# Attention logits in alternating row groups, with pairs of PSUM banks that also take the transposed probabilities

## Chip, cores, metric

One core of a Trainium2 chip. The metric is the device time of one execution in microseconds (us), and the number compared is the median over runs.

## What is computed

Two stacks of two layers each, on 256 tokens of 1024 channels in float32. The first stack mixes by three attentions (A: top-k by index scores, B: sliding window with sinks, C: stick-breaking), each with its own projections; the second works on two streams, x and a context c, with four mixers (A: a gated linear scan in both directions, B: dense GQA, C: differential attention, D: windowed GQA with sinks). The second layer of the second stack gives out only x. Cut to the parts that the change touches:

```python
def diff_attention(q, k, v, lam, lam_init, subln_g):       # mixer C: q, k [.., heads, 2, 32]
    scale = q.shape[-1] ** -0.5
    def block(qb):
        logits = jnp.einsum('bqhmd,bthmd->bhmqt', qb, k) * scale
        p = jax.nn.softmax(logits, axis=-1)
        w = p[:, :, 0] - lam * p[:, :, 1]
        return jnp.einsum('bhqt,bthd->bqhd', w, v)
...
def global_gqa(q, k, v, sink=None):                        # mixers B, D: heads of 64 channels
        logits = jnp.einsum('bqkgd,btkd->bkgqt', qb, k) * scale
        p = jax.nn.softmax(logits, axis=-1)                # with a sink: one more column
        return jnp.einsum('bkgqt,btkd->bqkgd', p, v)
...
def step(s, xs):                                           # mixer A: the scan
        att = jnp.einsum('bthk,bshk,btshk->bhts', qf, kf, decay)
        o = jnp.einsum('bthk,bkhv->bthv', qf * jnp.exp(bcum), s) + jnp.einsum('bhts,bshv->bthv', att, vf)
```

## The kernel before

Everything is in one class, `Net`. The residual streams lie channel-major. The large projections split their operands into a high and a low part (`split`, L111 on ScalarE and L112 on VectorE; tiles `wh`, `wl` of the weights, names such as `uh`/`ul`, `hxh`/`hxl`, `hch`/`hcl` of the activations) and take three products; `proj_tok` and `proj_ch` send 48 matmuls of 256 columns into one PSUM tile. These matmuls use the whole 128x128 array in one pass each. All other products are float32 and take two passes, which the trace shows as two records for each matmul.

PSUM has eight banks, in four pools: `pj` (3, projections), `lg` (2, logits and other short products), `tr` (2, transposes), `py` (1, the attention outputs). `mm` (L104) issues a matmul, `T` (L108) a transpose on TensorE.

A head has 64 channels, so its operands lie on partitions 0 to 63 or 64 to 127: the upper or the lower half of TensorE's rows, here called row group 0 and row group 1. An attention does, for one head or a few: the logits into an `lg` bank, for A, B and D with a mask added by one more matmul; `probs` (L397 the row maximum on VectorE, L402 exp with its sum on ScalarE); `weights_t` (L608 reciprocal, L610 scaling, transposes into a `tr` bank, L617 the copy `pt` to SBUF); then the products with the values into the `py` bank. It finishes one head (or the heads of one row group) before it begins the next. Mixer C has heads of two maps with 32 channels each: `diff` multiplies the queries by a mask (`qz`, L921) so that a product over all 128 rows gives one map's logits, combines both maps (L931 to L933), and transposes in `p_times_v` (copy `pt` at L412).

The scan (`gla`, L753 on) goes over levels b = 1, 2, 4 .. 128. A level copies the keys (`kc`, L794), does its products (`small` for b up to 16 in blocks of 32 columns, 128 columns above), picks values out of PSUM (L779, L811), and multiplies `QT`, `KT` and `FT` for the next level (L827, L829, L832).

A scheduler in the framework orders the instructions of every engine from its own estimates, so an edit at one place may move the rest. It runs waiting projections between the steps of attention and scan, as far as PSUM tiles are free.

Of the kernel before, what the change touches and what calls it, by code (L numbers as in the profile page):

```python
# [8 lines left out]
F32 = mybir.dt.float32  # L9
# [3 lines left out]
AF = mybir.ActivationFunctionType  # L13
# [14 lines left out]
def _ap(t, base, dims):  # L28
# [5 lines left out]
       ("cs32", (2, 2, 32)), ("dmask", (4,)))  # L34
# [24 lines left out]
class Net:  # L59
    """Residual streams are kept channel-major, [128 channels, 8, 256 tokens].  Operands of the large products are  # L60
    float32 values split exactly into two float32r parts (high, low); a product takes high*high + high*low + low*high."""
# [3 lines left out]
    def __init__(self, ctx, tc, I):  # L65
# [12 lines left out]
        self.tr = pool("tr", 2, space=ps)  # L78
# [6 lines left out]
    # ---------------------------------------------------------------- tiles  # L85
# [9 lines left out]

    def halves(self, name, tags):
        """a [128, 8, 256] tile in two pieces"""
        return Halves([self.K(name, [128, 4, 256], tag=t) for t in tags])
# [15 lines left out]
    # ------------------------------------------------------------ constants  # L114
    def load_consts(self):
# [9 lines left out]
        # 2 * silu of the conditioning vectors (ada halves its sums)  # L125
# [17 lines left out]
    def more_consts(self):  # L143
# [34 lines left out]
        # -lambda of the differential attention, per layer  # L178
# [13 lines left out]
        # forget gate lower bounds -> f = A + B * tanh(z / 2)  # L192
# [30 lines left out]
    def wtile(self, ap, c0, n=256, kt=8, pre=None):  # L223
        """columns c0..c0+n of ap [kt*128, N], split: w[part](k) -> [128, n]"""
# [16 lines left out]
    def fill(self, n, tags):  # L241
        """waiting jobs for a stretch in which the streams' chain leaves TensorE idle; their weights go to idle tags"""
# [5 lines left out]
    def proj_tok(self, w, n, u):  # L248
        """u (split, [128, 8, 256]) times w -> [128 tok, 2, n]"""
# [9 lines left out]
    def proj_ch(self, w, u, kt=8):  # L259
        """w (256 columns) times u -> [128 ch, 2, 256 tok]"""  # L260
# [9 lines left out]
    # --------------------------------------------------------------- pieces  # L270
    def ada(self, l, blk):
        """the modulation vectors, channel-major [128, 24, nv], and the jobs that fill them"""
# [9 lines left out]
        def job(n, ws=None):  # L282
# [8 lines left out]
            pc = self.P(self.tr, [128, 2, 4, 32])  # L291
# [9 lines left out]
    def chan_sum(self, x, square=False):  # L301
        """sums over channels of x [128, 8, 256] (or of its square), in four parts: rows 32 * g"""
        p = self.P(self.lg, [128, 512])
# [10 lines left out]
    def mean_row(self, x):  # L314
        """channel sums on every partition"""
        sb = self.chan_sum(x)
        p = self.P(self.lg, [128, 512])
# [3 lines left out]
    def rstd_row(self, x, eps):  # L321
        """(mean of x ** 2 over channels + eps) ** -0.5 on every partition"""
        V = self.nc.vector
        sb = self.chan_sum(x, True)
        p = self.P(self.lg, [128, 512])
# [13 lines left out]
    def log_exp(self, ins):  # L339
        """behind ins, ScalarE's tables hold both functions"""  # L340
# [4 lines left out]
    def rstd_small(self, r, ss):  # L345
        """(ss / 64 + eps) ** -0.5 of a few columns"""
# [3 lines left out]
    def rope(self, dst, src, H, cs, D=64, axial=False, dup=False):  # L350
        """src [128, 2, >=H*D] (PSUM or SBUF), dst [128, 2, H(, 2), D]; cs [128, 2 tok tiles, (cos, sin), D]"""
# [37 lines left out]
    def probs(self, hs, L, logits, nm, ss, nsink=None):  # L389
# [3 lines left out]
        p = self.P(self.lg, [128, nh, L])  # L393
        logits(p)
# [10 lines left out]
    def p_times_v(self, e, L, y, v):  # L405
# [25 lines left out]
    def affine_split(self, h, l, x, scale, bias, r=None):  # L431
        """split of x * scale (* r) + bias; scale and bias per channel, r per token"""
# [10 lines left out]
    def block1(self, l, xT, mod, pre):  # L443
# [18 lines left out]
        # ---- index scores, mixer A  # L462
# [24 lines left out]
        for t in range(2):  # L487
            L = 128 * (t + 1)
            S = self.W("score", [128, 256])[:, :L]
            rl = self.K("relu", [128, 4, 256], tag="at")  # L490
            for a in range(2):
                p = self.P(self.lg, [128, 2, 256])
                b = 64 * a
                for j in range(2):
                    self.mm(p[:, j, :L], iqT[b:b + 64, j, t * 128:t * 128 + 128], iqT[b:b + 64, 2, :L])
                A.activation(rl[:, a::2, :L], p[:, :, :L], AF.Relu)
# [32 lines left out]
        # ---- mixer C  # L529
# [10 lines left out]
        # ---- mixer B  # L540
# [49 lines left out]
    def finish1(self, ys, gT, Y):  # L590
        """gated and split"""
# [6 lines left out]
    def weights_t(self, e, hs, L, nm, ss, sink=None):  # L598
        """probabilities of heads hs from e [128 t, nh, L], transposed: [128 s, nh * L / 128, 128 t]"""
# [11 lines left out]
        p = self.P(self.tr, [128, 4, 128])  # L611
# [8 lines left out]
    def causal_softmax(self, H, tags, qT, kT, v, mask, sink=None, nsink=None):  # L620
        """causal tiles of 128 queries; mask(t) [128, L] additive bf16; -> [128 (head, channel), 4, 128 tok] each"""
        ys = []
        for t in range(2):
# [5 lines left out]
            for g in range(0, H // nh, 2):  # L629
                pts = []  # L630
                for a in range(2):
                    h0 = a + nh * g
                    hs = list(range(h0, h0 + 2 * nh, 2))

                    def logits(p):
                        for j, h in enumerate(hs):
                            b = 64 * (h % 2)
                            self.mm(p[:, j, :], qT[b:b + 64, h // 2, t * 128:t * 128 + 128], kT(h)[:, :L],
                                    start=j == 0, stop=False)
                        self.mm(p, self.identb, m[:, None, :L].to_broadcast([128, nh, L]), start=False, stop=True)  # L640
                    e = self.probs(hs, L, logits, nm, ss, nsink)
                    pts.append(self.weights_t(e, hs, L, nm, ss, sink))
# [10 lines left out]
    def stick(self, qT, kT, v, g, Y):  # L653
        """stick-breaking attention in [s, t] layout"""
        nc, V, A = self.nc, self.nc.vector, self.nc.scalar
        sl = [(slice(None), slice(None), slice(128 * s, 256)) for s in range(2)]
        for q in range(2):
            es = self.K("ste", [128, 4, 2, 256], tag="at")
            for a in range(2):
                b = 64 * a  # L660
                ps = []
                x = self.K("stx", [128, 768], tag=("s3", "n2")[a])
                xs = [x[:, :512].rearrange("p (j t) -> p j t", j=2), x[:, 512:].rearrange("p (j t) -> p j t", j=2)]
                for s in range(2):
                    p = self.P(self.lg, [128, 2, 256])
# [6 lines left out]
                    ps.append(p)  # L672
# [39 lines left out]
    def residual(self, n, r, g, b, name):  # L712
        """ALPHA * (n * r * g + b), put aside in DRAM until the layer's end"""
# [19 lines left out]
    def norm_layer(self, x):  # L733
        """x -> x - mean over channels; returns the rstd row"""
# [7 lines left out]
    def forget(self, l, d, p, FT, KT):  # L742
        """d: 0 forward, 1 backward; p [128, 2, 256] pre-activations"""
# [638 lines left out]
```

## Time and profile before

| | |
|---|---|
| runs (us) | 1384.69, 1383.55, 1381.17; median 1383.55 |
| profiled execution, span | 1377.40 us, one core, mean granted clock 0.986 |
| TensorE busy | 1330.4 us (97%) |
| VectorE / ScalarE / GpSimd busy | 844.3 (61%) / 655.1 (48%) / 25.4 us (2%) |
| DMA | 205.07 MB, 149 GB/s mean |

The span runs from the first to the last instruction of the profiled execution; the median of the runs is 6.15 us above it, and no device time beside the span was recorded for that execution. A busy time counts an engine as busy from an instruction's recorded start to its recorded end; on TensorE these overlap, and the recorded start of a matmul that follows another shape of tile lies ahead of the work. The distance between two starts therefore says more than a duration there.

### The profile page before, as it was taken

The numbers are of one execution on the slowest core, as the hardware profiler recorded it, in microseconds if no ns is written. First come the engines' busy times: TensorE is split into PE (matmuls) and PEld (weight loads), VectorE is DVE, ScalarE is ACT, GpSimd is POOL, SyncE is SP. The second block draws the span as 40 slices with busy tenths as digits, with TensorE's granted clock in tenths as the row PEclk, the third lists the DMA queues.
The fourth block names the chain that finished last, engine by engine and source line by source line (L and its number), as shares of the span: only waits on it lengthen the run. The fifth ranks groups of instructions, "written<-read, shape, count | busy, mean of one in ns | idle before, by whom it ended". The sixth has DMA issues, their size and how long they took to land.

```text
span 1377.4 us, 27990 instructions
## 1 busy us (share of the span) xinstructions
PE 1330.4 (97%) x11682; PEld 1164.2 (85%) x11682; DVE 844.3 (61%) x1744; ACT 655.1 (48%) x1178; POOL 25.4 (2%) x23
## 2 busy tenths in 40 slices
PE   5999999999999999999998999999999998999996
PEld 2998987899889898789998989977877788997774
DVE  3795454655559544565576366756577777775764
ACT  3455555544444545654443233346455546534652
POOL 0000000000000000000000000000000000000000
PEclk9899999999999999999999999999999999999998
DMA  9754746568746474547764442322143355522111
GB/s 330 216 151 131 232 142 190 158 204 266 227 124 184 123 212 141 153 138 220 211 214 153 135 142 63 109 93 77 52 139 118 107 154 159 175 81 62 62 62 46
DMA packets 199214, 205.07 MB, mean 149 GB/s; under 512 B 8368, under 2 KB 197424, under 8 KB 198448
## 3 DMA queue, kind: packets, MB, share of 16 engines
q1 hardware_dynamic: 199088, 203.28, 48.3%
q8 instruction: 92, 1.51, 0.4%
q14 instruction: 34, 0.28, 0.1%
HBM read 199.06 MB, written 4.19 MB: 148 GB/s over the span
## 4 chain that ended last, share of the span: by engine, by line
PE 82%; DMA 6%; DVE 4%; issue 4%; ACT 2%; SPq 1%; POOL 0%; POOLq 0%; ACTq 0%; DVEq 0%
PE ps L104 77%; PE ps L108 5%; DMA wr<-w_in 4%; DMA wsp<-w_ada 2%; DVE wl L112 2%; ACT wh L111 1%; SPq L219 1%; DMA wr<-w_out 0%; DMA cT<-ctx 0%; DVE KTc L829 0%; DVE af L439 0%; ACT Xx L1305 0%; ACT pe L402 0%; ACT L566 0%; DVE QTc L827 0%
## 5 line engine op out<-in xcount | busy, mean ns | idle before, releaser
L112 DVE TENSOR_TENSOR wl<-wr,wh 128x1024 fp32r<-128x1024 f32 (+1 forms) x270 | 328.4, 1217 | 258.3 <-ACT wh L111 255.8
L111 ACT ACTIVATE wh<-wr 128x1024 fp32r<-128x1024 f32 (+1 forms) x270 | 284.6, 1055 | 378.2 <-PE ps L104 255.2
L104 PE MATMUL ps<-uh,wh 128*128 128x256 f32 x704 | 202.2, 287 | 2.4 <-ACT thm L566 2.4
L104 PE MATMUL ps<-ul,wh 128*128 128x256 f32 x704 | 200.9, 285 | 0.0
L104 PE MATMUL ps<-uh,wl 128*128 128x256 f32 x704 | 200.8, 285 | 0.0
L104 PEld LDWEIGHTS ps<-uh,wh 128*128 128x128 f32 x704 | 132.7, 188 | 8.2 <-issue 4.4
L104 PEld LDWEIGHTS ps<-ul,wh 128*128 128x128 f32 x704 | 132.8, 189 | 1.9 <-issue 1.7
L104 PEld LDWEIGHTS ps<-uh,wl 128*128 128x128 f32 x704 | 132.7, 188 | 1.9 <-issue 1.6
L104 PE MATMUL ps<-wh,uh 128*128 128x256 f32 (+1 forms) x416 | 120.2, 291 | 2.0 <-ACT uh L440 1.2
L104 PE MATMUL ps<-wl,uh 128*128 128x256 f32 (+1 forms) x416 | 119.9, 289 | 1.0 <-DVE wl L112 1.0
L104 PE MATMUL ps<-wh,ul 128*128 128x256 f32 (+1 forms) x416 | 120.0, 289 | 0.1
L402 ACT ACTIVATE pe<-ps,nm 128x512 f32<-128x512 f32 (+2 forms) x160 | 84.9, 539 | 54.4 <-DVE nm L397 41.1
L397 DVE TENSOR_REDUCE nm<-ps 128x1 f32<-128x512 f32 (+2 forms) x104 | 71.1, 687 | 42.2 <-PE ps L104 42.0
L104 PEld LDWEIGHTS ps<-wh,uh 128*128 128x128 f32 x416 | 81.2, 196 | 4.1 <-ACT uh L440 1.4
L104 PEld LDWEIGHTS ps<-wl,uh 128*128 128x128 f32 x416 | 81.3, 196 | 1.8 <-DVE wl L112 1.3
L104 PEld LDWEIGHTS ps<-wh,ul 128*128 128x128 f32 x416 | 81.5, 196 | 1.2 <-DVE ul L441 0.9
L104 PE MATMUL ps<-wh,hxh 128*128 128x256 f32 x256 | 72.4, 283 | 0.0
L104 PE MATMUL ps<-wh,hxl 128*128 128x256 f32 x256 | 72.1, 281 | 0.0
L104 PE MATMUL ps<-wl,hxh 128*128 128x256 f32 x256 | 72.0, 281 | 0.0
L104 PE MATMUL ps<-hxh,wh 128*128 128x256 f32 x224 | 64.9, 294 | 4.2 <-ACT hxh L440 4.2
L104 PE MATMUL ps<-hxl,wh 128*128 128x256 f32 x224 | 64.6, 290 | 2.7 <-DVE hxl L441 2.7
L104 PE MATMUL ps<-hxh,wl 128*128 128x256 f32 x224 | 64.6, 290 | 0.6 <-DVE wl L112 0.6
(351 smaller groups left out, 3150.7 us busy)
## 6 DMA issues: line engine op xcount, KB each, us to landing
wr<-w_in SPq DMA_DIRECT2D x204, 512.0 KB, 4.0
wsp<-w_ada SPq DMA_DIRECT2D x68, 512.0 KB, 5.7
wr<-w_out SPq DMA_DIRECT2D x40, 512.0 KB, 3.7
wr<-w_ada SPq DMA_DIRECT2D x28, 512.0 KB, 3.9
wr<-w_br_a SPq DMA_DIRECT2D x8, 512.0 KB, 3.9
wr<-w_br_c SPq DMA_DIRECT2D x8, 512.0 KB, 4.6
wr<-w_br_b SPq DMA_DIRECT2D x8, 512.0 KB, 4.6
Xx<-resx SPq DMA_DIRECT2D x2, 1024.0 KB, 4.7
```

The source lines that it names most:

```text
L104: self.nc.tensor.matmul(o, l, r, start=start, stop=stop, skip_group_check=True)
L108: self.nc.tensor.transpose(o, i, self.ident[:n, :n])
L111: self.nc.scalar.activation(h, x, AF.Copy)
L112: self.nc.vector.tensor_tensor(l, x, h, op=OP.subtract)
L219: self.nc.sync.dma_start(out=w[:, :, :n], in_=ap[k0 * 128:k0 * 128 + 512, c0:c0 + n].rearrange("(k p) n -> p k n", p=128))
L397: nc.vector.tensor_reduce(nmx, p, axis=AX.X, op=OP.max, negate=True)
L402: nc.scalar.activation(e[:, j, :], p[:, j, :], AF.Exp, bias=nm[:, h:h + 1], accum_out=ss[:, h:h + 1])
```

## The change

The pool `tr` is gone, and `lg` has two tiles of two banks each (`P2`). `banks` issues the logits of the row groups alternately, each group into its own bank, and the masks behind them. The probabilities are transposed into the bank that held their own logits (`blocks`). The other users of `tr` (`tok_to_ch`, `finish2`, the modulation vectors in `ada`, the scan's state tiles) take tiles of `pj`. `chan_sum`, `mean_row` and `rstd_row` take a pair and use one half. Mixer C's queries are no longer masked: each map's logits use 32 rows, and the scale 32 ** -0.5 goes into the copy of the queries in `tok_to_ch`. Maps of 256 keys, which shared a bank, now have one each. In the scan, the loop over row groups becomes the inner one.

```diff
+    def P2(self, *shape):
+        t = self.lg.tile([128, 2, 512], F32, name="pp")
...
-        self.tr = pool("tr", 2, space=ps)
...
     def tok_to_ch(self, dst, src, scale=1.0, n=2):
-        p = self.P(self.tr, [128, 2, 2, 128])
+        p = self.P(self.pj, [128, 2, 2, 128])
...
+    def banks(self, nh, L, q, k, mask=None):
+        ps = self.P2(nh, L)
+        for j in range(nh):
+            for a, p in enumerate(ps):
+                self.mm(p[:, j, :], q(a, j), k(a, j), start=j == 0, stop=mask is None)
+        if mask is not None:
+            for p in ps:
+                o, m = mask(p)
+                self.mm(o, self.identb, m, start=False, stop=True)
+        return ps
...
-    def weights_t(self, e, hs, L, nm, ss, sink=None):
+    def weights_t(self, e, hs, L, nm, ss, p, sink=None):
...
-        p = self.P(self.tr, [128, 4, 128])
+        p = self.blocks(p)
...
     def small(lhs, rh, first, mask):
-            for a in range(2):
-                p = self.P(self.lg, [128, 2, 2, 32])
-                for ct in range(2):
-                    for t in range(2):
+            ps = self.P2(2, 2, 32)
+            for ct in range(2):
+                for t in range(2):
+                    for a in range(2):
...
             for h in range(4):
-                qz = self.W("qz", [128, 2, 128])
...
-                V.tensor_tensor(qz, qT[:, ct:ct + 1, t * 128:t * 128 + 128].to_broadcast([128, 2, 128]),
-                                self.dmask[:, mo:mo + 2, None].to_broadcast([128, 2, 128]), op=OP.mult)
...
+                rows = [slice(64 * (h % 2) + 32 * m, 64 * (h % 2) + 32 * m + 32) for m in range(2)]
+                ps = self.banks(1, L, lambda m, j: qT[rows[m], ct, t * 128:t * 128 + 128],
+                                lambda m, j: kT[rows[m], ct, k0:k0 + L])
+                es = [self.probs([2 * h + m], L, ps[m], nm, ss)[:, 0] for m in range(2)]
```

On TensorE, at the end of mixer C of the last layer (`pe` are probabilities, `pt` the SBUF copy of their transpose, `vC` values, `kC` keys, `qz` the masked and `qC` the plain queries). Before:

```order
L104 MATMUL ps_14629<-vC_14147,pt_14735 128x64 x4
L104 MATMUL ps_14800<-kC_13165,qz_14798 128x512
L108 MATMUL ps_14760<-ident_111,pe_14749 128x128 x4
L104 MATMUL ps_14805<-kC_13165,qz_14798 128x512
L104 MATMUL ps_14629<-vC_14147,pt_14765 128x64 x4
L104 MATMUL ps_14827<-kC_13165,qz_14825 128x512
L108 MATMUL ps_14787<-ident_111,pe_14776 128x128 x4
```

The change, in the same place:

```order
L117 MATMUL pp_14585<-kC_13020,qC_13846 128x512 x2
L121 MATMUL pp_14562<-ident_108,pe_14566 128x128 x4
L117 MATMUL ps_14463<-vC_13993,pt_14579 128x64 x4
L117 MATMUL pp_14608<-kC_13020,qC_13846 128x512 x2
L121 MATMUL pp_14585<-ident_108,pe_14589 128x128 x4
L117 MATMUL ps_14463<-vC_13993,pt_14602 128x64 x4
```

The two maps' logits stand together now, and the product with the values (`vC,pt_14579`) stands right behind the transposes of the same probabilities (`pp_14562`, which `pt_14579` is copied from), where a logits product stood between.

On TensorE, the scan of x in the last layer (`QTx`, `kc`: queries and copied keys; `wh`, `hch`, `hxh` and the like: projections). Before, a level:

```order
L104 MATMUL ps<-wh,hch 128x256
L104 MATMUL ps<-wh,hcl 128x256
L104 MATMUL ps<-wl,hch 128x256
L104 MATMUL ps<-QTx,kc 32x32 x32
L104 MATMUL ps<-wh,hch 128x256
L104 MATMUL ps<-wh,hcl 128x256
```

The change:

```order
L117 MATMUL ps<-wh,hxh 128x256
L117 MATMUL ps<-wh,hxl 128x256
L117 MATMUL ps<-wl,hxh 128x256
L117 MATMUL pp<-QTx,kc 32x32 x119
L121 MATMUL ps<-ident,ro 128x128 x4
L117 MATMUL ps<-wh,hxh 128x256
```

A level has 32 such products. Before, projections stand between any two levels; now three levels and most of a fourth stand in a row, and the rest of that fourth with two more behind the projections that follow (a row of 73).

## Rows read from the trace of the kernel before

**Rows 1.** The page: busy time, share of the span and instructions of each engine.
```profile
PE 1330.4 (97%) x11682; PEld 1164.2 (85%) x11682; DVE 844.3 (61%) x1744; ACT 655.1 (48%) x1178; POOL 25.4 (2%) x23
```

**Rows 2.** Stretches: length, busy PE, PEld, DVE, ACT, POOL (instructions), granted clock, DMA share, GB/s.
```profile
0.00:40.00 40.00, 24.69 (x186) 11.60 (x187) 18.32 (x71) 15.00 (x28) 0.91 (x5) 0.89 1.01 327
...
600.00:640.00 40.00, 40.00 (x350) 38.00 (x349) 20.96 (x31) 17.76 (x24) 0.00 (x0) 1.00 0.60 180
...
1200.00:1240.00 40.00, 40.00 (x557) 37.15 (x555) 29.80 (x60) 14.15 (x22) 0.00 (x0) 1.00 0.29 83
...
1280.00:1320.00 40.00, 39.71 (x237) 28.37 (x236) 31.23 (x83) 24.00 (x59) 1.81 (x1) 1.00 0.17 54
```

**Rows 3.** Timeline of PE around logits of 512 keys, 64 rows: start, us, what.
```profile
916.42 0.28 PE L104 MATMUL ps<-hcl,wh 128*128 128x256 f32 x1
916.63 1.12 PE L104 MATMUL ps<-kB,qB 64*128 64x512 f32 x2
917.68 0.39 PE L104 MATMUL ps<-hch,wl 128*128 128x256 f32 x1
917.91 0.28 PE L104 MATMUL ps<-hch,wh 128*128 128x256 f32 x1
```

**Rows 4.** Timeline of PE: logits of 256 keys (three, then two), projections between.
```profile
904.84 1.13 PE L104 MATMUL ps<-kB,qB 64*128 64x256 f32 x6
905.91 1.05 PE L104 MATMUL ps<-wr,cs 128*32 128x256 f32 x10
...
907.23 0.28 PE L104 MATMUL ps<-hch,wl 128*128 128x256 f32 x1
...
909.47 0.28 PE L104 MATMUL ps<-hch,wh 128*128 128x256 f32 x1
909.68 1.13 PE L104 MATMUL ps<-kB,qB 64*128 64x256 f32 x4
910.74 0.39 PE L104 MATMUL ps<-hcl,wh 128*128 128x256 f32 x1
```

**Rows 5.** Timeline of PE at mixer C, last layer, masked queries, and the transposes.
```profile
1288.04 1.02 PE L104 MATMUL ps<-kC,qz 128*128 128x512 f32 x2
1288.89 1.00 PE L104 MATMUL ps<-vC,pt 128*128 128x64 f32 x8
1289.73 0.61 PE L108 MATMUL ps<-ident,pe 128*128 128x128 f32 x4
```

**Rows 6.** Timeline of PE, one level of the scan.
```profile
1206.90 0.28 PE L104 MATMUL ps<-wl,hch 128*128 128x256 f32 x1
1207.11 0.76 PE L104 MATMUL ps<-QTx,kc 64*32 64x32 f32 x64
1207.80 0.38 PE L104 MATMUL ps<-wh,hch 128*128 128x256 f32 x1
1208.02 0.28 PE L104 MATMUL ps<-wh,hcl 128*128 128x256 f32 x1
```

**Rows 7.** Timeline of DVE behind a level of the scan (its products start at 1212.76).
```profile
1213.29 0.60 DVE L779 COPY_PREDICATED gc<-c_gmask,ps 128x128 f32<-128x128 uint8 x2 [2.31 <-PE ps L104]
1213.79 0.68 DVE L827 TENSOR_TENSOR QTx<-QTx,FTx 128x512 f32<-128x512 f32 x1
1214.51 0.28 DVE L832 TENSOR_TENSOR FTx<-FTx 128x64 f32<-128x64 f32 x1
1214.89 0.69 DVE L829 TENSOR_TENSOR KTx<-KTx,FTx 128x512 f32<-128x512 f32 x1
```

**Rows 8.** Timeline of DVE and ACT (two answers) between logits and products, mixer C, last layer.
```profile
1289.09 0.69 DVE L397 TENSOR_REDUCE nm<-ps 128x1 f32<-128x512 f32 x1 [1.07 <-PE ps L104]
...
1291.08 0.75 DVE L933 SCALAR_TENSOR_TENSOR pe<-pe,dc 128x512 f32<-128x512 f32 x1
...
1289.82 0.69 ACT L402 ACTIVATE pe<-ps,nm 128x512 f32<-128x512 f32 x1 [2.01 <-DVE nm L397]
...
1290.50 0.59 ACT L412 ACTIVATE pt<-ps 128x512 f32<-128x512 f32 x1
```

More of the change, by code (lines that the diff above doesn't have):

```diff
@@ L94, in P @@
         return pool.tile(shape, dt, name="ps")
+    def P2(self, *shape):
+        t = self.lg.tile([128, 2, 512], F32, name="pp")
+        n = math.prod(shape)
+        out = []
+        for a in range(2):
+            v = t[:, a, :n]
+            if len(shape) == 2:
+                v = v.rearrange("p (a b) -> p a b", a=shape[0])
+            elif len(shape) == 3:
+                v = v.rearrange("p (a b c) -> p a b c", a=shape[0], b=shape[1])
+            out.append(v)
+        return out
     def halves(self, name, tags):
@@ L403, in probs, with blocks, p_times_v @@
         return e
-    def p_times_v(self, e, L, y, v):
+    @staticmethod
+    def blocks(p):
+        return _ap(p, p, [[128, 4], [1, 128]])
+    def p_times_v(self, e, L, y, v, p):
         nst = L // 128
-        p = self.P(self.tr, [128, 4, 128])
+        p = self.blocks(p)
         for s in range(nst):
@@ L490, in block1 @@
             rl = self.K("relu", [128, 4, 256], tag="at")
-            for a in range(2):
[L492 to L496, printed above, removed]
+            ps = self.P2(2, 256)
+            for j in range(2):
+                for a in range(2):
+                    b = 64 * a
+                    self.mm(ps[a][:, j, :L], iqT[b:b + 64, j, t * 128:t * 128 + 128], iqT[b:b + 64, 2, :L])
+            for a in range(2):
+                A.activation(rl[:, a::2, :L], ps[a][:, :, :L], AF.Relu)
             V.tensor_scalar(S, rl[:, 0, :L], iws[:, t, 0:1], None, op0=OP.mult)
@@ L633, in causal_softmax @@
                     hs = list(range(h0, h0 + 2 * nh, 2))
[L635 to L642, printed above, removed]
+                    e = self.probs(hs, L, ps[a], nm, ss, nsink)
+                    pts.append(self.weights_t(e, hs, L, nm, ss, ps[a], sink))
                 for j in range(nh):
@@ L798, in gla @@
             elif out:
-                for a in range(2):
-                    p = self.P(self.lg, [128, 2, 2, 128])
-                    for ct in range(2):
-                        for t in range(2):
+                ps = self.P2(2, 2, 128)
+                for ct in range(2):
+                    for t in range(2):
+                        for a, p in enumerate(ps):
                             h = 2 * ct + a
@@ L809, in gla @@
                                         QT[64 * a:64 * a + 64, 1 - t, ct, 128 * (1 - t):128 * (1 - t) + 128])
+                for a, p in enumerate(ps):
                     if b < 128:
@@ L889, in gqa @@
             pts = {}
-            for hs in ([[0, 2], [1, 3]] if nh == 2 else [[h] for h in range(4)]):
-                def logits(p):
-                    for j, h in enumerate(hs):
-                        b = 64 * (h % 2)
-                        self.mm(p[:, j, :], qT[b:b + 64, h // 2, t * 128:t * 128 + 128],
-                                kT[b:b + 64, h // 2, k0:k0 + L], start=j == 0, stop=masks is None)
-                    if masks is not None:
-                        m, st = masks[t]
-                        self.mm(p[:, :, 128 * st:128 * st + 128], self.identb, m, start=False, stop=True)
-                e = self.probs(hs, L, logits, nm, ss, nsink)
-                pt = self.weights_t(e, hs, L, nm, ss, sink)
-                for j, h in enumerate(hs):
-                    pts[h] = pt[:, j * nst:j * nst + nst]
-                if h % 2:
-                    for c in range(h // 2 if nh == 1 else 0, h // 2 + 1):
-                        for s in range(nst):
-                            for a in range(2):
-                                self.mm(y[64 * a:64 * a + 64, c, 128 * t:128 * t + 128], v(c, s),
-                                        pts[2 * c + a][:, s], start=s == 0, stop=s == nst - 1)
+            mask = None
+            if masks is not None:
+                m, st = masks[t]
+                mask = lambda p: (p[:, :, 128 * st:128 * st + 128], m)
+            for cs in ([[0, 1]] if nh == 2 else [[0], [1]]):
+                ps = self.banks(nh, L, lambda a, j: qT[64 * a:64 * a + 64, cs[j], t * 128:t * 128 + 128],
+                                lambda a, j: kT[64 * a:64 * a + 64, cs[j], k0:k0 + L], mask)
+                for a in range(2):
+                    hs = [2 * c + a for c in cs]
+                    e = self.probs(hs, L, ps[a], nm, ss, nsink)
+                    pt = self.weights_t(e, hs, L, nm, ss, ps[a], sink)
+                    for j, h in enumerate(hs):
+                        pts[h] = pt[:, j * nst:j * nst + nst]
+                for c in cs:
+                    for s in range(nst):
+                        for a in range(2):
+                            self.mm(y[64 * a:64 * a + 64, c, 128 * t:128 * t + 128], v(c, s),
+                                    pts[2 * c + a][:, s], start=s == 0, stop=s == nst - 1)
         self.nc.scalar.activation(ys().rearrange("p (c n) -> p c n", c=2), y, AF.Copy)
@@ L1079, in qk_c @@
                 A.activation(f2(ro), p, AF.Copy)
-            self.tok_to_ch(dst, f2(ro))
+            self.tok_to_ch(dst, f2(ro), scale)
         def mixer_c(s):
@@ L1361, in _constants @@
     out["gmask64"] = top(p ^ q, 64).astype(f)
-    out["dmask"] = np.where(p // 32 == np.arange(4)[None], 32 ** -0.5, 0).astype(f)
     pack = lambda names: np.ascontiguousarray(np.concatenate([out[n].reshape(128, -1) for n in names], 1))
```

48 lines of the change are left out of this document (21 added, 27 removed).

## The prediction

> **What bounds the kernel now.** I read the page first: TensorE (PE) is busy for 97% of the span, VectorE for 61%, ScalarE for 48% [rows 1]. Then the stretches of 40 us: from 40 us on PE is at 39 to 40 of 40 nearly everywhere, at a granted clock of 1.00, whether a stretch holds projections alone, a scan or mixer C; only the first stretch stands out, where the transfers take all of the DMA time [rows 2]. So a microsecond less of PE work should be a microsecond less of time, as long as PE still finds other work when it would have to wait.
>
> PE's busy time doesn't say how long its work takes, since records overlap; for that I took distances between starts from the timeline. Projections follow one another in (909.47 - 907.23) / 19 = 0.118 us [rows 4]. A float32 product of 512 columns and 128 rows takes two passes of 0.43 us (1288.04 to 1288.89) [rows 5]. A product of 64 rows costs more than its passes: between the projection before (ends 916.42 + 0.12 = 916.54) and the second one behind (starts 917.91, so the first began its work at 917.79) lie 1.25 us, 0.86 of them passes [rows 3]. The other 0.39 are two changes of tile shape, **0.195 us each**. With these units the instructions of the kernel before add up to about 1312 us, 492 shape changes in it. The other 65 us of the span are waits: some 24 in the first stretch, 4 to 6 at each of three norms, the rest at the end. In attention and scan there are almost none: before, the work between the steps covers every chain.
>
> That two row groups run at the same time is in this trace already: three logits of 256 keys, one of them of the other row group, take 1.07 us to the next instruction, two of one row group 1.06 [rows 4]. The third costs nothing.
>
> **What the change takes off PE.** In the order of before, nearly all logits of a row group stand alone or beside their own kind; in the changed order they alternate. I counted passes that must follow one another.
> - 512 keys, 64 rows (B and D): 30 serial products become 18; 12 x 0.86 = 10.3 us.
> - 256 keys, 64 rows (first stack's A and B, its index scores, stream c): 25 fewer x 0.43 = 10.7 us; the 0.43 is a quarter of 1.06 less 0.2, twice [rows 4].
> - 128 columns: half of that, 0.216 each; 18 fewer in attention, and 3 in each of 9 scan products (0000 2222 has a serial length of seven, alternated four): 45 x 0.216 = 9.7 us.
> - Scan in blocks of 32: a level takes 1208.02 - 0.12 - 1207.02 = 0.88 us, 0.49 of it passes [rows 6]. At the best half goes; I take 0.22 x 18 levels = 4 us, bounds 0 and 4.5.
> - Mixer C: 32 products of 512 keys stand one after the other, now two maps side by side: 16 x 0.86 = 13.7 us; 256 keys, 8 x 0.43 = 3.4 us. Here the rows show concurrency for groups of 64 rows alone; for 32 rows the bounds are 0 and 17 us. I take 17, by the nearest row [rows 4].
> - Modulation vectors' products are less interrupted: 2 us. Shape changes fall from 492 to 424, although mixer C now adds some: 68 x 0.195 = 13.3 us.
>
> Together about **67 us** off PE (1312 to 1245).
>
> The Trainium skill (TensorE: Matmul & The Clock Gate, section "Wait — 56ns, not 53.3ns?") says that matmuls never start less than about 25 ns apart, however few their columns; by that, alternation gives nothing in the 32-column levels and the sum would be 4 us smaller. The trace disagrees: 64 records between 1207.11 and 1207.80 are 10.8 ns apart [rows 6].
>
> VectorE loses the 24 query multiplications, and gets twice as many, half as long, maxima for the 256-key maps. It isn't the bound, so I cost both at nothing; the cover is PE's own work, and where that is missing they are inside the waits below.
>
> **What the change adds: waits.** With `tr` gone, `tok_to_ch`, the scan's state tiles and `finish2` compete with projections for three `pj` banks, so projections can't run ahead as they did; and a transpose needs the bank of its own logits. What is then late is in the order:
> - Scan. Before, at least 2.2 us of other work stand between two levels, typically 4. In the changed order 12 transitions have nothing between. PE must then wait for VectorE: pick 0.60, queries 0.68, and in a run of levels also gates 0.28 and keys 0.69, 2.25 us in all [rows 7], of which PE's next level hides about 0.4. Lower bound: 1.1 (the products began at 1212.76, took about 0.6, and the queries were done at 1214.47). Upper bound 3.3, when a weight split gets between. I take 1.7: **20 us**, bounds 13 and 40. Projections, transposes and all later steps queue behind the waiting level, as PE works in order.
> - Products with the values directly behind their own transposes. From the transposes' start to the end of the copy `pt` it is 1290.50 + 0.59 - 1289.73 = 1.36 us [rows 5, 8]; transposes take 0.44, so 0.92 is bare. 19 places of 88 have less than 1.0 us between (before: 5), in sum 13 us short. Bounds 6 and 23.
> - From logits to transposes: maximum 0.69, exp with its sum 0.88, combination 0.75 and small steps, 1289.09 to 1291.83 in a row with no second map to wait for [rows 8]; with the second map's maximum and exp it is 3.9 to 4.2. Before, the least cover was 4.3 us; now a dozen places have 1.5 to 3.5, 16 us short in sum, of which the waits in the line above already give about 7. I take 9, bounds 3 and 22.
> - Reuse of a bank soon after its last write: 29 places under 1.4 us (before 6), most by little: 4 us, bounds 0 and 8.
>
> Waits together: 20 + 13 + 9 + 4 = **46 us**. The other waits (start, norms, end) stay. 67 - 46 = 21 us less: the profiled execution's span goes from 1377.4 to 1356.4 us, and with the 6.15 us by which the median of the runs lies above that span, **1363 us**.
>
> **Rivals.**
> 1. The waits are mostly absorbed: each scan transition costs its lower bound, 13 us, and attention and banks together 10, because the second row group's bank is ready while the first is worked on. 67 - 23 = 44 less: 1340 us. For it: before, VectorE has 9 to 10 us idle in each 40 in these stretches [rows 2]. Against: PE's order is fixed, and nothing stands in the gaps. Chance 0.20.
> 2. **Slower:** the serial chain through VectorE and ScalarE takes the place of PE as the bound wherever PE has no filler. The 12 scan transitions at 3.3 (40 us), 17 more value products at the whole 1.36 (23), logits to transposes 16, less 2 that exist now, 5 for banks: 82 us, 15 more than the gain, 1398 us. It decides from 71 us of waits on. For it: VectorE is busy for 29.8 and 31.2 of 40 us in the last layer's scan and mixer C [rows 2], so chains there meet weight splits. Against: in the changed order most steps still have projections between. Chance 0.20. The Trainium skill (TensorEngine Tiling (Array Packing), section "PSUM Bottleneck") warns of this: tiling speeds up TensorE, not the emptying of PSUM. No stretch of before shows it, as PE is above 39 us of 40 there.
> 3. The change doesn't do what it says in mixer C: products of 32 rows don't run side by side. Then 17 us of the gain are missing: 1380 us. For it: no row shows such tiles; against: groups of 64 rows do it [rows 4]. Chance 0.07.
>
> My forecast has the remaining 0.53.
>
> **How the numbers follow.** About 0.3%, 4 us, is what a measurement of this kernel can tell from no change. The forecast case runs from 1350 to 1378 with small spill, rival 1 around 1340, rival 3 about at the edge, rival 2 from 1385 to 1400. The range 1338 to 1392 holds the forecast, most of rival 1, rival 3 and the lower part of rival 2. Faster: 0.53 less a spill of 0.05, plus 0.20, plus 0.02 of rival 3: 0.70. Same: 0.04 of that spill, 0.04 of rival 3, 0.04 of rival 2: 0.12. Slower: the rest, 0.18.
>
> **What would show it.** Right: pairs of 512-key logits, mixer C's included, take about 1.06 us to the next start; scan levels take about 0.2 us less; PE's idle time is in the last layer's scan and in mixer C, released by VectorE's `QT` and ScalarE's `pt`; projections' rate is unchanged. Mixer C's pairs at 1.7 us or more show rival 3; PE under 36 us of 40 in the scan stretches shows rival 2. It is wrong if alternating row groups don't overlap in general, or if waits appear in projections (late weights), which I cost at nothing.

## The result, and the profile after

The changed kernel takes **1566.25 us** (median of four runs, 1563.57 to 1573.59), the kernel before 1382.36 us: a ratio of 1.1338, 95% interval 1.1306 to 1.137. It is slower by 184 us, where 1363 us had been forecast.

The page of the changed kernel, busy time of each engine (to be held against [rows 1]):

```profile
PE 1359.7 (87%) x11682; PEld 1197.0 (76%) x11682; DVE 845.4 (54%) x1728; ACT 659.0 (42%) x1179; POOL 27.0 (2%) x23
```

The span has grown by 1566.4 - 1377.4 = 189 us. PE's idle time has gone from 1377.4 - 1330.4 = 47 us to 1566.4 - 1359.7 = 207, so 160 us of it are waits. The other 29 us are more *busy* time, although as many matmul records as before (11682) are there and the promised overlap is there too. That overlap first; the timeline of PE in the changed kernel, logits of 512 keys in 64 rows, then mixer C's in 32 rows:

```profile
1014.29 1.13 PE L117 MATMUL pp<-kB,qB 64*128 64x512 f32 x4
1015.35 0.66 PE L121 MATMUL ps<-ident,ro 128*128 128x128 f32 x4
...
1446.04 1.13 PE L117 MATMUL pp<-kC,qC 32*128 32x512 f32 x4
1447.10 0.38 PE L117 MATMUL ps<-hxh,wl 128*128 128x256 f32 x1
```

Two logits now take 1.06 us to the next start, as one did before (1.05, [rows 3]), with 32 rows as with 64. So rival 3 is out, and the largest terms of PE's gain are there; the scan's part is looked at under hybrid_scan. Where the time goes is in the view of lines, PE alone, each shape apart (after the bar: busy us, mean ns, idle time of PE just before them and who ended it):

```profile
L121 PE MATMUL ps<-ident,ro 128*128 128x128 f32 x152 | 33.6, 341 | 75.8 <-DVE ro L392 41.2 <-DVE ro L390 17.6 <-DVE ro L1081 11.3
L121 PE MATMUL ps<-ident,adas 128*128 128x128 f32 x96 | 22.9, 324 | 25.9 <-ACT adas L303 22.6 <-DVE rec L639 3.0
L117 PE MATMUL pp<-QTx,kc 64*32 64x32 f32 x768 | 10.6, 221 | 16.6 <-ACT kc L821 9.3 <-DVE QTx L855 5.0 <-ACT th L1052 2.3
L121 PE MATMUL pp<-ident,pe 128*128 128x128 f32 x336 | 58.1, 293 | 14.1 <-DVE pe L641 9.8 <-DVE pe L953 4.2
```

The largest is none of the forecast's terms: 76 us ahead of the transposes of rotated queries and keys (`ro`, in `tok_to_ch`), and 26 ahead of those of the modulation vectors (`adas`). In the same view of the kernel before these groups have 0.5 and 2.8 us. The timeline shows what happens there; PE, changed kernel, first layer:

```profile
47.52 0.64 PE L121 MATMUL ps<-ident,ro 128*128 128x128 f32 x4 [2.56 <-DVE nlam L203]
47.91 0.36 PE L117 MATMUL ps<-wh,uh 128*128 128x256 f32 x1
...
53.49 0.27 PE L117 MATMUL ps<-wl,uh 128*128 128x256 f32 x1
57.73 1.08 PE L121 MATMUL ps<-ident,ro 128*128 128x128 f32 x4 [3.97 <-DVE ro L392]
58.47 0.41 PE L117 MATMUL ps<-wh,uh 128*128 128x68 f32 x1
58.69 0.41 PE L117 MATMUL ps<-wh,ul 128*128 128x68 f32 x1
```

A projection runs from 47.91 to 53.6; then PE stands until 57.73 for VectorE to rotate just that projection (with a weight split of 1.2 us between its steps), transposes it, and only then starts the next one. The instruction order of both kernels tells why: in every pool the tiles' first writes stand on PE in the order in which the program asks for the tiles, without one exception (214 tiles in `pj` and 187 in `tr` before; 313 in `pj` after). Program order is projection, transpose, projection. While the transposes had a pool of their own, the next projection could be issued ahead of the transpose; in one pool it can't.

The last rows show the second cost: the steps between matmuls of 68 columns are 0.21 us, where the kernel before takes 0.11 at the full clock. The stretches say what the clock is (columns as in [rows 2]):

```profile
40.00:80.00 40.00, 30.46 (x191) 29.87 (x191) 14.23 (x39) 7.90 (x12) 0.00 (x0) 0.71 0.40 123
...
440.00:480.00 40.00, 29.84 (x193) 28.90 (x194) 14.95 (x32) 10.22 (x15) 0.00 (x0) 0.74 0.30 82
...
1320.00:1360.00 40.00, 26.39 (x541) 25.13 (x540) 27.48 (x59) 13.43 (x22) 2.64 (x2) 0.74 0.30 88
```

Where PE waits, the granted clock falls too, from 1.00 to a mean of 0.71 to 0.74, a mix of the two levels of 2.4 and 1.2 GHz; over the whole span it is 0.909 instead of 0.986. In the trace's clock records the low level lasts 285 us instead of 39. 491 projection matmuls start in it instead of 82, and at 0.213 us a step instead of 0.118 they take 36 us longer than those of before. In all, PE is busy for 206 us at the low level instead of 28; at half speed, half of the difference, some 90 us, is what the clock costs (an estimate). With it the sum nearly closes: 67 us less work by the order, 160 us more waits and 90 us for the clock make 183 of the 189 us.

### The profile page after: what moved, and what is told of

Read it like the earlier page. It is cut to its first block, busy times and chain, and to the rows that moved or that the text cites. A ratio compares the mean times of both kernels' runs of the same rounds, so it can differ in the third digit from the quotient of the medians.

```text
span 1566.4 us, 27937 instructions
## 1 busy us (share of the span) xinstructions
PE 1359.7 (87%) x11682; PEld 1197.0 (76%) x11682; DVE 845.4 (54%) x1728; ACT 659.0 (42%) x1179; POOL 27.0 (2%) x23
## 4 chain that ended last, share of the span: by engine, by line
PE 39%; DVE 7%; issue 5%; DMA 5%; ACT 4%; POOL 1%; POOLq 0%; SPq 0%; ACTq 0%; DVEq 0%
PE ps L117 31%; PE pp L117 4%; DMA wr<-w_in 4%; DVE wl L125 2%; ACT wh L124 2%; PE ps L121 2%; PE pp L121 2%; DMA wr<-w_out 1%; ACT pe L426 1%; POOL rec L361 1%; DVE nm L421 0%; DMA cT<-ctx 0%; DVE KTc L857 0%; DVE rt L378 0%; ACT pt L441 0%
## 5 line engine op out<-in xcount | busy, mean ns | idle before, releaser
L117 PE MATMUL ps<-wh,uh 128*128 128x256 f32 (+1 forms) x416 | 131.4, 316 | 0.3 <-ACT wh L124 0.3
L117 PE MATMUL ps<-wh,ul 128*128 128x256 f32 (+1 forms) x416 | 129.4, 311 | 1.2 <-DVE ul L470 1.2
L426 ACT ACTIVATE pe<-pp,nm 128x512 f32<-128x512 f32 (+2 forms) x160 | 84.7, 536 | 68.3 <-DVE nm L421 46.6
L421 DVE TENSOR_REDUCE nm<-pp 128x1 f32<-128x512 f32 (+3 forms) x112 | 72.1, 650 | 75.4 <-ACT pt L648 36.8
L121 PE MATMUL ps<-ident,ro 128*128 128x128 f32 x152 | 33.6, 341 | 75.8 <-DVE ro L392 41.2
L117 PEld LDWEIGHTS ps<-wh,ul 128*128 128x128 f32 x416 | 91.3, 219 | 3.7 <-DVE ul L470 2.5
L117 PEld LDWEIGHTS ps<-wh,uh 128*128 128x128 f32 x416 | 91.4, 220 | 2.5 <-issue 1.8
L117 PEld LDWEIGHTS ps<-wl,uh 128*128 128x128 f32 x416 | 90.8, 218 | 2.0 <-DVE wl L125 1.9
L121 PEld LDWEIGHTS ps<-ident,ro 128*128 128x128 f32 x152 | 20.7, 167 | 87.6 <-issue 65.0
L121 PE MATMUL pp<-ident,pe 128*128 128x128 f32 x336 | 58.1, 293 | 14.1 <-DVE pe L641 9.8
```

Of the source, the lines that this page charges most:

```text
L117: self.nc.tensor.matmul(o, l, r, start=start, stop=stop, skip_group_check=True)
L121: self.nc.tensor.transpose(o, i, self.ident[:n, :n])
L421: nc.vector.tensor_reduce(nmx, p, axis=AX.X, op=OP.max, negate=True)
L426: nc.scalar.activation(e[:, j, :], p[:, j, :], AF.Exp, bias=nm[:, h:h + 1], accum_out=ss[:, h:h + 1])
```

## Experiments

TensorE's work "by the order" is counted as in the prediction (1312 us before, 1245 us after). Two theories stood at the start: **order** (one pool for projections and transposes puts them into program order) and **capacity** (three banks are too few for both).

| run | TensorE work by the order | median us | ratio to before, 95% interval |
|---|---|---|---|
| moved_only | 1297 | 1551.29 | 1.1234 (1.1211 to 1.1256) |
| before_one_pool | 1296 | 1620.91 | 1.1745 (1.1721 to 1.177) |
| two_plus_one | 1249 | 1438.05 | 1.0421 (1.0397 to 1.0444) |
| own_bank | 1248 | 1448.19 | 1.0499 (1.0481 to 1.0517) |
| own_bank_states | 1253 | 1434.95 | 1.0407 (1.0377 to 1.0438) |
| one_pair_tr | 1258 | 1454.80 | 1.0549 (1.0524 to 1.0574) |
| own_one_pair_tr | 1254 | 1455.23 | 1.0536 (1.0513 to 1.0559) |
| own_bank_masked | 1262 | 1424.51 | 1.0313 (1.0296 to 1.0331) |
| own_bank_dummy | 1287 | 1428.80 | 1.0352 (1.0337 to 1.0368) |
| hybrid | 1294 | 1363.61 | 0.9872 (0.9856 to 0.9889) |
| hybrid_scan | 1284 | 1361.07 | 0.9853 (0.9837 to 0.987) |
| hybrid_inbank | 1295 | 1473.56 | 1.07 (1.066 to 1.074) |

### One edit alone, and the same banks split or merged

moved_only is the kernel before with these lines (also in `ada`, `finish2` and the scan's states):

```diff
     def tok_to_ch(self, dst, src, scale=1.0, n=2):
-        p = self.P(self.tr, [128, 2, 2, 128])
+        p = self.P(self.pj, [128, 2, 2, 128])
```

> The kernel before with one part of the change: tok_to_ch, the modulation vectors, the scan's state tiles and finish2 take banks of the projections' pool; the probabilities keep the transposes' pool, and logits, masks and banks stay as before. Order theory: this edit alone carries nearly all of the loss, 1500 to 1600 us, with the mean granted clock near 0.91. Rival (the loss comes from the attentions, where pairs and transposes in the logits' own banks hold banks longer): 1385 to 1430 us.

1551 us: put into the kernel before by itself, this edit costs 171 us, at a clock of 0.924. Its view of lines has the wait again:

```profile
L108 PE MATMUL ps<-ident,ro 128*128 128x128 f32 x152 | 35.2, 356 | 67.0 <-DVE ro L379 34.9 <-DVE ro L377 14.3 <-DVE ro L1061 11.9
```

before_one_pool takes no bank away at all:

```diff
-        self.pj = pool("pj", 3, space=ps)
+        self.pj = pool("pj", 5, space=ps)
...
-        self.tr = pool("tr", 2, space=ps)
+        self.tr = self.pj
```

> The kernel before with its projections' pool of three and its transposes' pool of two made one pool of five; nothing else. Order theory: projections now stand behind every earlier transpose, those of the probabilities too: 100 to 200 us slower than before, at a lower mean clock. Capacity theory: five banks that anybody may take are at least as good: within 1% of before.

1621 us, worse than the order theory asked, with 79.4 us idle ahead of the transposes of `ro`. Five banks for all are much worse than three and two. The other way round, two_plus_one leaves the changed kernel its three banks and splits them (the former users of `tr` go back to it):

```diff
-        self.pj = pool("pj", 3, space=ps)
+        self.pj = pool("pj", 2, space=ps)
+        self.tr = pool("tr", 1, space=ps)
```

> The changed kernel, with the same three banks split: two for projections, one for the transposes and state tiles that had come to the projections' pool. Order theory: what waits is set by the shared order, so most of the loss goes though no bank is added: 1400 to 1480 us. Capacity theory: 1550 us or more, since projections have fewer banks still.

1438 us, 128 less than the change, without a bank more. The wait is gone as well:

```profile
L122 PE MATMUL ps<-ident,ro 128*128 128x128 f32 x152 | 26.2, 290 | 2.6 <-DVE adar L309 2.1 <-DVE ro L1068 0.3
```

Capacity is out; order holds.

### Transposes in their projections' own banks

```diff
-    def tok_to_ch(self, dst, src, scale=1.0, n=2):
-        p = self.P(self.pj, [128, 2, 2, 128])
+    def tok_to_ch(self, dst, src, p, scale=1.0, n=2):
+        p = _ap(p, p, [[256, 2], [128, 2], [1, 128]])
```

(`p` is the projection's tile, whose values have been rotated into SBUF by then; the modulation vectors' transposes take the free half of their bank.)

> The changed kernel, but the transposes of tok_to_ch and of the modulation vectors go into the bank of their own projection, so they take no bank of the pool. Order theory (a pool hands out its banks in program order, so that no projection can start ahead of an earlier transpose that takes a bank of the same pool, and TensorE waits for the rotation on VectorE): the 85 us at the transposes of ro and the 33 us at those of the modulation vectors go, and a good half of what the slow clock costs behind them, some 30; about 1415 us, between 1390 and 1450. Capacity theory (three banks are too few for projections and transposes together): each bank is now held longer, from the projection to the copy behind the transposes, so no gain, 1560 us or more.

(The view of lines above gives 76 and 26 us for these two waits.)

1448 us, within the range. In its view of lines the idle time ahead of `ro` is 12.8 us and ahead of `adas` 5.8. The first stack now ends 19 us earlier than in the kernel before (first projection of x in the second stack at 710.7 us instead of 729.9), with 15 us of idle time up to there instead of 21. What is left lies in the second stack. own_bank_states moves the scan's states and `finish2` as well:

```diff
-                    p = self.P(self.pj, [128, 2, 2, 128])
+                    p = self.P2(2, 2, 128)[0]
```

> As own_bank, and the scan's state tiles and the transposes of finish2 take half a pair of the logits' pool instead of a bank of the projections' pool. Order theory: projections can now run between the levels of the scan again, and of the 42 us of waits at the scan's products most go, with some of the clock: about 1365 us, between 1335 and 1400, 25 to 60 us less than own_bank. Rival (the scan waits since its levels are bound by VectorE whatever stands around them): within 15 us of own_bank.

13 us less, 1435. Ahead of the scans' products of 32 columns the changed kernel idles for 16.6 us in stream x and 9.8 in c, own_bank for 0.0 and 10.3, and this one for 0.0 and 0.5: where projections stand between the levels again, VectorE no longer holds them up. But that was not the rest of the loss: the range (1335 to 1400) was missed, and by the number, though not by the mechanism, the rival was right. (The view of lines gives 33 us, not 42, for all of the changed kernel's waits at the scan's products.) The timeline of PE in this kernel, mixer C of the last layer:

```profile
1308.32 2.08 PE L117 MATMUL pp<-kC,qC 32*128 32x512 f32 x4
1310.33 1.11 PE L121 MATMUL pp<-ident,pe 128*128 128x128 f32 x4
1312.49 1.97 PE L117 MATMUL ps<-vC,pt 128*128 128x64 f32 x8 [1.04 <-ACT pt L441]
1314.39 2.08 PE L117 MATMUL pp<-kC,qC 32*128 32x512 f32 x4
```

No projection stands in this stretch (from 1297 to 1339 us, 41 us; before, 36 us with 84 projection matmuls among them). A round takes 1314.39 - 1308.32 = 6.07 us, in which PE waits 1.04 us for the copy `pt`, and everything runs at the low clock: the logits take 2.01 us instead of 1.06.

### Which part of the attention

If a bank that is blocked until its transposes are copied out is the cause, a pool for the transposes should help, with one pair for logits:

```diff
-        self.lg = pool("lg", 2, space=ps)
+        self.lg = pool("lg", 1, space=ps)
+        self.tr = pool("tr", 2, space=ps)
...
-        p = self.blocks(p)
+        p = self.P(self.tr, [128, 4, 128])
```

> The changed kernel with one pair of banks for logits instead of two, and the two banks so gained made the transposes' pool of the kernel before again, for all its former users, the probabilities included. The order counts 1258 us of TensorE work, 54 less than before. Bank theory (what is left to lose, beside the shared projections' pool, is that a pair is blocked from its logits to the copy of its own transposes, so that products with the values and next logits wait): most of the 110 us of waits left in own_bank_states go, 1340 to 1375 us, faster than before. Rival (once alternation has made TensorE's part short, the second stack's attentions are bound by the chain through VectorE and ScalarE, whichever bank the transposes use; one pair even shortens the lookahead): 1400 to 1440 us.

> As one_pair_tr, but the rotated projections and the modulation vectors are transposed in their own projections' banks, so that the transposes' pool serves probabilities, state tiles and finish2 alone. Bank theory: the shared order of the transposes' pool (rotated projections behind earlier probabilities) costs a little; 5 to 20 us faster than one_pair_tr. Rival: own banks hold projections' banks longer, same as one_pair_tr within 5 us or slower.

(In own_one_pair_tr the rotated projections keep their own banks.) 1455 us both, above the ranges of both sides. The bank theory in this form fell, and where the rotated projections are transposed makes no difference here. But one pair of banks is also one less than the changed kernel has, and mixer C of the last layer has no projections beside it either. So these two runs can't separate the parts. hybrid_inbank, further down, does.

own_bank_masked gives mixer C its masked queries back, in own_bank_states:

```diff
-                ps = self.banks(1, L, lambda m, j: qT[rows[m], ct, t * 128:t * 128 + 128],
-                                lambda m, j: kT[rows[m], ct, k0:k0 + L])
+                ps = self.banks(1, L, lambda m, j: qz[:, m], lambda m, j: kT[:, ct, k0:k0 + L])
```

> own_bank_states with mixer C's logits as before: masked queries over all 128 rows, two serial products a pair, everything else kept. TensorE's work by the order rises by 9 us (1253 to 1262), less than the 17 of the passes, as the shape changes fall. If mixer C is bound by TensorE's work, 9 to 12 us slower than own_bank_states. If it is bound by the chain through ScalarE and VectorE, the second product lies in the waits: within 5 us.

It is 10 us *faster*, which neither side expected; the mean clock is 0.961 instead of 0.942. own_bank_dummy adds work without any use:

```diff
+                for _ in range(2):
+                    self.mm(ps[1][:, 0, :], qT[:, ct, t * 128:t * 128 + 128], kT[:, ct, k0:k0 + L])
                 self.p_times_v(es[0], L, y[:, 4 * t + h], lambda s, h=h: v(h, s), ps[0])
```

> own_bank_states with two useless float32 products of the full array per head of mixer C, into the second map's bank behind its exp, ahead of the transposes; 34 us more TensorE work at the full clock. Clock theory (in mixer C of the last layer the granted clock is 0.58 since TensorE idles half of a round, and a round of 6.07 us consists of work at half speed as much as of waits): with the gaps filled the clock stays up, a round falls below 5.5 us, and the whole is no slower or up to 25 us faster than own_bank_states. Rival (the clock costs little, a round is as long as its chain through VectorE and ScalarE): a round is longer than 6.07 us and the whole 10 to 35 us slower.

34 us more work on PE, 6 us less time, clock 0.97. Its timeline has two rounds between 1326.94 and 1337.59:

```profile
1326.94 0.60 PE L121 MATMUL pp<-ident,pe 128*128 128x128 f32 x4
...
1337.59 0.60 PE L121 MATMUL pp<-ident,pe 128*128 128x128 f32 x4
```

5.3 us a round with two more products in it: the low clock was part of the round, as the clock theory says. By the clock records PE is busy at the low level for 62 us here, 86 in own_bank_masked and 132 in own_bank_states. Half of what fell away, 35 us here and 23 there, is by this estimate what the clock gives back, against 34 and 9 us of added work. The 6 us themselves are at the edge of the noise: own_bank_states ran from 1429.7 to 1438.9 us, this kernel from 1428.0 to 1430.5. The waits at VectorE and ScalarE remain, and the whole stays 3.5% above before.

### The first stack changed, the second as before

hybrid closes the PSUM pools between the stacks and opens those of before (`NetB` is the class of the kernel before; the first stack is that of own_bank):

```diff
+    N.pctx.close()
+    N.__class__ = NetB
+    for name, bufs in (("pj", 3), ("lg", 2), ("tr", 2), ("py", 1)):
+        setattr(N, name, N.pctx.enter_context(tc.tile_pool(name=name + "2", bufs=bufs, space=bass.MemoryType.PSUM)))
```

> First stack as in own_bank (alternating row groups, pairs, transposes in their own banks); then the PSUM pools are closed and opened anew, and the second stack is the kernel before, instruction for instruction. If the gain of alternation is real where projections cover the chains, the first stack ends 19 us earlier, as in own_bank, and nothing else changes: 1362 us, between 1352 and 1372. If the end of the first stack only shifts waits into the second, 1375 us or more.

1363.61 us, faster than before by 1.3%: of the 18 us of work that the order saves in the first stack, 17 arrive, since there projections cover the chains. hybrid_scan lets the second stack's scan alternate its row groups as well, with tiles of `lg` and `tr` as before:

> As hybrid, and the second stack's scan alternates its row groups too, into the two single banks of the logits' pool. By the order 10.6 us less TensorE work than hybrid. If the scan is covered by projections: 1352 us, 8 to 12 less than hybrid. If the scan is bound by VectorE: within 3 us of hybrid.

**1361.07 us**, the lowest of all, 1.5% below before. But it is 2.5 us less than hybrid, not 8 to 12, and the two intervals overlap; by the number the rival was right. PE's timeline says why. First a level of 32-column products in hybrid_scan, as in [rows 6]; then products of 128 columns, before and in hybrid_scan:

```profile
1188.71 0.28 PE L1307 MATMUL ps<-wl,hch 128*128 128x256 f32 x1
1188.92 0.76 PE L1307 MATMUL ps<-QTx,kc 64*32 64x32 f32 x64
1189.83 0.28 PE L1307 MATMUL ps<-wh,hcl 128*128 128x256 f32 x1
...
1220.89 0.28 PE L104 MATMUL ps<-wl,hxh 128*128 128x256 f32 x1
1221.10 1.71 PE L104 MATMUL ps<-QTx,kc 64*128 64x128 f32 x16
1222.96 0.28 PE L104 MATMUL ps<-wh,hxl 128*128 128x256 f32 x1
...
1204.12 0.28 PE L1307 MATMUL ps<-wl,hxh 128*128 128x256 f32 x1
1204.33 1.16 PE L1307 MATMUL ps<-QTx,kc 64*128 64x128 f32 x16
1205.64 0.28 PE L1307 MATMUL ps<-wh,hxl 128*128 128x256 f32 x1
```

Reckoned as in the prediction, the level takes 1189.83 - 0.12 - 1188.83 = 0.88 us, exactly as before: in blocks of 32 columns alternation saves nothing. The products of 128 columns take 1.28 us instead of 1.83, 0.55 less where three times 0.216 had been forecast. Nine of these would give some 5 us in place of the 10.6 by the order. PE also idles for 38 us instead of hybrid's 33; 1.3 us of that lie ahead of the scan of c, the rest is spread over the kernel and not explained.

hybrid_inbank puts one part of the change into the second stack of hybrid, with single banks, masked queries and the logits' order of before:

```diff
-        p = self.P(self.tr, [128, 4, 128])
+        p = self.blocks(self.bank)
```

(in `p_times_v` and `weights_t`; `self.bank` is the bank of the logits)

> As hybrid, with one part of the change put into the second stack: the probabilities are transposed into the bank of their own logits (two single banks, logits, masks and queries as before; the transposes' pool stays for all other users). Its order has the same TensorE work as hybrid (1295 us), but no projection left beside mixer C's products of the last layer (hybrid: 84). Bank theory (a bank that is held from the logits to the copy of the transposes halves the lookahead in the second stack's attentions): 1390 to 1440 us, with waits at the transposes and the products with the values of mixers C and D and a lower clock there. Rival (what the attentions of own_bank_states lose is due to the pairs and the alternation): 1358 to 1370 us.

1474 us, 110 more than hybrid by this edit alone, even above its range. The timeline of PE, mixer C of the last layer:

```profile
1332.85 1.12 PE L1304 MATMUL ps<-kC,qz 128*128 128x512 f32 x2 [1.60 <-ACT pe L1602]
1334.09 0.66 PE L1308 MATMUL ps<-ident,pe 128*128 128x128 f32 x4
1336.06 1.10 PE L1304 MATMUL ps<-vC,pt 128*128 128x64 f32 x8 [1.31 <-ACT pt L1613]
1337.00 1.08 PE L1304 MATMUL ps<-kC,qz 128*128 128x512 f32 x2
1339.73 1.13 PE L1304 MATMUL ps<-kC,qz 128*128 128x512 f32 x2 [1.65 <-ACT pe L1602]
```

A round takes 1339.73 - 1332.85 = 6.88 us. Both maps' logits, the transposes and the products with the values wait for one another through two banks. In the stretches:

```profile
1280.00:1320.00 40.00, 40.00 (x304) 33.95 (x303) 18.70 (x34) 16.59 (x29) 1.64 (x1) 1.00 0.26 79
1320.00:1360.00 40.00, 24.67 (x124) 12.72 (x122) 18.11 (x36) 14.59 (x33) 0.00 (x0) 1.00 0.08 27
```

Mixer B (up to 1324 us) still has projections beside it, 175 matmuls of them (hybrid: 81). Mixer C then has none (hybrid: 84), and PE is busy for 24.67 of 40 us, at the full clock: here the waits cost all by themselves. Over the whole run PE idles for 100 us instead of 33, and the low level lasts 111 us instead of 49 in hybrid_scan. The longer hold of the banks and the missing projections come with the same edit; what each of them costs was not separated.

## Why the prediction was wrong

- **What PE saves: right in the main.** Pairs of 512-key logits take 1.06 us, mixer C's included, so that rival 3 is out. In the first stack, where projections cover the chains, 17 of 18 us arrive (hybrid). But the scan's levels don't take 0.2 us less, as the prediction's own sign asked: they take 0.88 us before and after, so that this term, 4 us, is nothing. For the second stack no time shows the rest of the 67 us.
- **The step that failed is the sum of the waits, 46 us, and in it the reading of `tr`'s removal.** The prediction said that `tok_to_ch` and others now compete with projections for `pj`, "so projections can't run ahead as they did", and then priced this only at the scan (20 us) and as "reuse of a bank" (4 us). What it didn't price is the transpose of a rotated projection that stands directly behind that projection: 152 transposes, with 76 us of idle time ahead of them, and 26 us at the modulation vectors. The order showed it, but the places that were counted there were logits, scan levels and values alone. moved_only shows that this edit by itself costs 171 us, and two_plus_one that the changed kernel gets 128 us back when the transposes have a pool again.
- **Scan, 20 us:** too small. In the view of lines the scans' products wait 13 times where 12 had been counted, for 33 us in all, inside the bounds of 13 and 40. That they wait for want of other work was right: in own_bank_states, in which projections fill in again, these waits are gone. But the chain was too short: 9.3 of the 16.6 us ahead of x's 32-column products end with ScalarE's copy of the keys (`kc`, 0.64 us a copy), which stands behind VectorE's keys and had no place in the 2.25 us. PE's timeline of the changed kernel has three levels in a row, 2.4 to 3.1 us apart, where 2.1 had been reckoned (0.4 of work, 1.7 of wait):

```profile
1325.84 0.76 PE L117 MATMUL pp<-QTx,kc 64*32 64x32 f32 x64
1328.89 0.83 PE L117 MATMUL pp<-QTx,kc 64*32 64x32 f32 x64 [2.30 <-ACT th L1052]
1331.29 0.88 PE L117 MATMUL pp<-QTx,kc 64*32 64x32 f32 x64 [1.56 <-DVE QTx L855]
```

- **Attention, 13 + 9 us:** the mechanism was right, the size wrong. In the changed kernel 14 us of idle time stand ahead of the transposes of probabilities and 13 ahead of the value products; when the larger loss is taken away, own_bank_states shows 22 and 28 us there (before: 2 in all). The prediction counted each gap of the order by itself, with the cover that the scheduler had planned. On the chip, a wait also delays what stands behind it, so that mixer C becomes a loop through two pairs. hybrid_inbank prices the transposes in the logits' banks alone at 110 us, clock included, where only two single banks are there.
- **The clock was taken as given.** It fell from 0.986 to 0.909, some 90 us by the estimate above, and no term of the sum stands for it. "Projections' rate is unchanged" was wrong for some 400 of 7392 matmuls.
- **The 6.15 us** between span and median are no fixed term: the profiled execution of the changed kernel took 1568.23 us at a span of 1566.4.
- **Rival 2** had the right direction, but the larger part of its mechanism was missing: it put all waits at scan and attention and came to 1398 us. Its sign, PE under 36 us of 40 in the scan, did come (26.39 from 1320 to 1360 us), but that stretch holds waits for `ro` as well, so the sign can't tell the two apart. Its page, TensorEngine Tiling (Array Packing) in the Trainium skill, section "PSUM Bottleneck", says that tiling doesn't speed up the emptying of PSUM; hybrid_inbank and mixer C of own_bank_states agree as far as PE's waits there end with ScalarE reading a bank (2.9 of a round of 6.88 us, 1.0 of 6.07). It says nothing of the larger cost, the order that a shared pool imposes.

## What to carry to other kernels

When a change merges buffer pools, look first for what may no longer overtake what: the banks were enough, the order was not (before: five in one pool 1621 us, three and two 1380; changed: three in one pool 1566, two and one 1438). Price every chain that lost its cover in the new order, not only those that the change is about. A gain of the bound engine is worth its full size only where other work covers the chains; this one paid in the first stack, and every kernel tried that has all of it in the second stack is slower than before.

## What the hardware showed that was not expected

- Products of 32 rows in two row groups run side by side: four passes of 512 columns in 1.06 us to the next start.
- The same alternation gains by size: products of 128 columns went from 1.83 to 1.28 us, levels of 32-column products stayed at 0.88. Why the small ones gain nothing was not tried.
- More work can be faster: 9 us of masked products took 10 us off, and 34 us of useless products cost no time, both with a higher mean clock (0.961 and 0.97 against 0.942).
- A loop with waits doesn't always lose its clock: from 1320 to 1360 us, where mixer C runs in both, own_bank_states ran at 0.58 with PE busy for 35.13 of 40 us, hybrid_inbank at 1.00 with 24.67. Counted at the full clock, the round of hybrid_inbank holds more work, two logits products one after the other (0.85 us each, [rows 5]) where own_bank_states has a pair in 1.06. What decides between them was not tried.
